# The last row block of a hybrid decoder block: column halves in PSUM tiles of their own, and a planner that takes a PSUM tile as one

## The chip, the cores and the metric

The kernel runs on one core of a Trainium2 chip. Such a core has five engines that run side by side and wait for each other through semaphores: TensorE (PE in the profile, with its weight loads as PEld), VectorE (DVE), ScalarE (ACT), GpSimd (POOL) and SyncE (SP, which here only starts transfers). Matmul results land in PSUM, a small memory of banks; everything else lives in SBUF. The metric is the device time of one execution in microseconds (us). Lower is better.

## The reference

One decoder layer over 1024 positions and 1024 channels, in float32. What matters for the text below is the middle of it:

```python
u = rms_norm(h, mix_pre_g)
z = einsum('bsd,de->bse', u, w_in)            # pooled part, q, k, v, two gates
ya = pool_mixer(p) @ w_branch_a
yb = diff_attention(q, k, v) @ w_branch_b
m = sigmoid(gate_a) * ya + sigmoid(gate_b) * yb
h = h + rms_norm(m @ w_out, mix_post_g)       # "row blocks" below
u = rms_norm(h, ffn_pre_g)
f = silu(u @ w_ffn_gate) * (u @ w_ffn_up)
h = h + rms_norm(f @ w_ffn_down, ffn_post_g)
```

## The kernel before

Every matrix product is made of three matmuls on operands that were split in a high and a low part (`triple`, lines 1056 to 1058: high by high, high by low, low by high), and many are seven-product schemes on 512x512 quarters. In the profile a triple is three rows of PE, one for each of those lines.

The work goes through these stages: the input projection, a part called the mixer (branch A, attention, branch B, the output projection with the residual and the second norm, and the first products of the FFN), the FFN's gate and up products, and the down projection with the last norm.

The mixer is not written in the order in which it runs. `mixer` lists tasks, each with an engine, an estimated duration, the slots it reads (`r=`) and writes (`w=`) and a rank. `Plan.op` makes a graph of them: a task goes behind those that wrote what it reads, and behind those that touched what it writes. A slot may be named with a key, `(o, e)`, and then only tasks with the same key are ordered. For PSUM slots (the pools in `BANKS`: "mm" and "fil" of two tiles of one bank, "pair" of two tiles of two banks) also two readers on different engines are ordered. `Plan.schedule` then gives each engine its order by those estimates, and `Plan.emit` writes the instructions down in the order of the planned starts. The semaphores are not the planner's: the layer below adds them while the instructions are written down, from the tiles that each touches, and it takes a whole tile as one, without the planner's keys. Each engine then works through its list in that order, and an instruction that waits holds all that stand behind it on the same engine.

Two places matter here.

Branch B (`block` and the loop around it, lines 582 to 605). For each of 16 blocks PE makes four triples into a "fil" tile `branch`; DVE multiplies it with a gate (`sgs <- branch, sgs`, after which the bank is free for the block after next) and adds the result to the accumulator `ma`; ahead of that DVE multiplies `ma` with the other gate. For the last four blocks (n of 12 to 15) the gates still need their sigmoid, on ACT, and the first one carries a load of ACT's function table. ACT also splits the branch's weights (`wb_hi`) and DVE makes their low part (`wb_lo`). Then come the weights of the output projection, `wo_raw`, `woh` and `wol`.

The row blocks (`row` for blocks 0 to 6, `last_row` for block 7). PE makes the row block's product `wo` of 128x1024 in a "pair" tile, ACT sums its squares (`sumsq`, into `junk`), DVE multiplies it with the gain (`og`), POOL takes the power for the norm, DVE adds the residual (`xr`), and the same again for the second norm; then PE transposes `og` (`turned`, tile `h_t`), and ACT and DVE make the FFN's operands of it. In blocks 0 to 6 both column halves (e of 0 and 1) are done by one instruction, in block 7 one after the other: eight triples for half 0, then eight for half 1. Between the triples of half 1 PE has the transposes of block 6, and behind them come FFN products (`Y`, `Z`) that need only the first four row blocks, while the norm of block 7 runs on the other engines; then the transposes of block 7.

Of the kernel before, what the change touches and what calls it, by code (L numbers as in the profile page):

```python
# [75 lines left out]
class Plan:  # L76
# [20 lines left out]
    def op(self, engine, cost, fn, r=(), w=(), rank=0.0, size=0.0, claim=(), chain=None, behind=None,  # L97
# [156 lines left out]
def mixer(pl, k):  # L254
# [331 lines left out]
    for n, (d, t) in enumerate(order):  # L586
# [11 lines left out]
        if (1, d) in (k.unfinished if k else [(1, 6), (1, 7)]):  # L598
            pl.op("ACT", act(HALF) + .2, lambda sg=sg: A.activation(sg()[:, 1], sg()[:, 1], AF.Sigmoid),
                  w=[(sg, 1)], rank=r0)  # L600
# [69 lines left out]

    def row_products(o, mh, ml, kb, e, rank):
        hi, lo = wo[kb // 2]

        def fn():
            c = slice(e * HALF, (e + 1) * HALF)
            wh, wl = hi()[:, kb % 2, c], lo()[:, kb % 2, c]
            k.triple(o()[:, e, :], mh()[:, kb, :], ml()[:, kb, :], wh, wl, kb == 0, kb == KD - 1, False)
        return pl.op("PE", TRIPLE, fn, r=[(mh, kb // 2), (ml, kb // 2), (hi, kb % 2), (lo, kb % 2)], w=[(o, e)],
                     rank=rank, chain="fill")

    def turned(tb, og, rank):
        last, h, c = tb == NB - 1, *divmod(tb, 4)
        both = bank("pair", "h_t") if last else None
        for kq in (1, 0) if last else (0, 1):
            pt = both if last else bank("mm", "h_t")
            view = (lambda kq=kq, pt=pt: pt()[:, kq, :]) if last else pt
            key = (pt, kq) if last else (pt, None)

            def fn(kq=kq, view=view):
                for i in range(4):  # L690
                    at = kq * 4 + i
                    nc.tensor.transpose(view()[:, i * P:(i + 1) * P], og()[:, at * P:(at + 1) * P], k.ident)
            done = pl.op("PE", 4 * .109, fn, r=[(og, kq)], w=[key], rank=3000.0)
            v = lambda view=view: view().rearrange("p (k t) -> p k t", k=4)
            src = v, [key], HALF, False
            raw = raws[h][kq]
            if last and kq == 1:
                both_parts(A2, [c], rank - 1, src)
            pl.op("ACT", act(HALF), lambda raw=raw, v=v: A.copy(raw()[:, :, cols(c)], v()), r=[key], w=[(raw, c)],
                  rank=rank)  # L700
# [44 lines left out]
    def last_row():  # L745
        tb, rank = NB - 1, 100.0 + 10 * (NB - 1)
        mh, ml, xr = operands(tb, rank - 18)
        o, og = bank("pair", "wo"), b4([P, D], F32, "og", "row")
        c = [slice(0, HALF), slice(HALF, D)]
        ss, ms, r = small(4, "hss"), small(4, "ms"), small(2, "rstd")  # L750
        for e in range(2):
            for kb in range(KD):
                last7[0] = row_products(o, mh, ml, kb, e, 4000.0 + tb)
            pl.op("ACT", act(HALF) + .23, lambda e=e: k.sumsq(o()[:, e, :], ss()[:, e:e + 1]), r=[(o, e)], w=[(ss, e)],
                  rank=URGENT)
            pl.op("DVE", dve(HALF), lambda e=e: tt(og()[:, c[e]], o()[:, e, :], gpost()[:, c[e]], ALU.mult),
                  r=[(o, e), gpost], w=[(og, e)], rank=URGENT)
        mean(ms, ss, 0, URGENT)
# [959 lines left out]
```

## Time and profile before

| | |
|---|---|
| median of 3 runs | 1254.37 us (1252.97 to 1255.44) |
| the profiled execution | 1254.28 us |
| its span, first to last instruction | 1252.5 us |
| PE busy | 1237.7 us, 99% of the span |
| DVE, ACT, POOL busy | 839.9, 583.9, 142.7 us |
| chain that ended last | PE 95%, DMA 2%, ACT 1%, DVE 1% |

A row of the timeline is: start, duration, engine, source line, instruction, tiles written and read, shapes, count, and in brackets how long the engine had been idle before it and what ended that. Consecutive instructions of one kind are merged to one row. Matmul rows overlap: a row's duration runs to the end of its result, while the next matmul starts earlier. Buffer numbers are left out of the names, so `wo` is the product of any row block and `junk <- wo` any sum of squares over it. `A_lo`, `S_lo`, `A_hi`, `u` around the row blocks are the FFN operands that ACT and DVE make from the transposed rows.

### The profile page before, as it was taken

To read this page: it belongs to the slowest core of one execution; us is meant where nothing else is said; L and a number is where in the kernel's file an instruction comes from. 1 tells how busy PE (TensorE), PEld (TensorE's weight loads), DVE (VectorE), ACT (ScalarE), POOL (GpSimd) and SP (SyncE) were. 2 spreads that over 40 slices of the span, in tenths; PEclk is the share of its full clock that TensorE was granted. 3 is DMA by queue.
4 is the path that set the end of the run, shared out by engine and by line. 5 is a ranking of instruction groups with operands and counts; after the bars stand their busy time and mean duration, and the time that the engine had idled before them with its cause. 6 is when DMAs were issued, how large, how long until landed. Compare 5 with 4: busy or idle time off the path is not lost.

```text
span 1252.5 us, 15725 instructions
## 1 busy us (share of the span) xinstructions
PE 1237.7 (99%) x5900; PEld 1038.0 (83%) x5900; DVE 839.9 (67%) x1314; ACT 583.9 (47%) x1051; POOL 142.7 (11%) x128
## 2 busy tenths in 40 slices
PE   8999999999999999999999999999999999999997
PEld 8888888888899998788788888888888888888886
DVE  5976776445399888885795655655645547955666
ACT  7543344434478773464553333333333333554552
POOL 4100000000201100010002111111111012000222
PEclk9999999999999999999999999999999999999999
DMA  8475336333693027572442332332332368733236
GB/s 253 148 235 192 139 120 221 106 130 118 222 381 136 18 71 266 187 262 89 145 158 87 124 126 85 93 104 98 127 102 98 113 213 278 247 94 107 78 109 210
DMA packets 139548, 190.69 MB, mean 152 GB/s; under 512 B 7632, under 2 KB 90320, under 8 KB 137040
## 3 DMA queue, kind: packets, MB, share of 16 engines
q1 hardware_dynamic: 127904, 159.15, 38.6%
q10 hardware_dynamic: 11568, 30.54, 6.4%
q8 instruction: 46, 0.75, 0.3%
q14 instruction: 30, 0.25, 0.1%
HBM read 128.06 MB, written 61.60 MB: 151 GB/s over the span
## 4 chain that ended last, share of the span: by engine, by line
PE 95%; DMA 2%; ACT 1%; DVE 1%; issue 0%; POOL 0%; SPq 0%; POOLq 0%; DVEq 0%; ACTq 0%
PE Y L1056 10%; PE Y L1058 10%; PE Y L1057 10%; PE X L1056 5%; PE X L1058 5%; PE X L1057 5%; PE Yd L1056 3%; PE Yd L1058 3%; PE Yd L1057 3%; PE Z L1058 3%; PE Z L1056 3%; PE Z L1057 3%; PE s L276 3%; PE o L276 3%; PE wo L1056 2%; PE wo L1058 2%
## 5 line engine op out<-in xcount | busy, mean ns | idle before, releaser
L1007 DVE TENSOR_TENSOR p<-Z,p 128x512 f32<-128x512 f32 x33 | 22.8, 692 | 166.1 <-PE Z L1058 162.5
L1056 PE MATMUL Y<-S_hi,Wh 128*128 128x512 f32 x288 | 112.3, 390 | 0.7 <-ACT p L1092 0.7
L1056 PE MATMUL X<-S_hi,Wh 128*128 128x512 f32 x288 | 112.3, 390 | 0.0
L1058 PE MATMUL Y<-S_hi,Wl 128*128 128x512 f32 x288 | 112.2, 389 | 0.0
L1057 PE MATMUL Y<-S_lo,Wh 128*128 128x512 f32 x288 | 112.1, 389 | 0.0
L1057 PE MATMUL X<-S_lo,Wh 128*128 128x512 f32 x288 | 112.0, 389 | 0.0
L1058 PE MATMUL X<-S_hi,Wl 128*128 128x512 f32 x288 | 112.0, 389 | 0.0
L1056 PE MATMUL Y<-A_hi,Wh 128*128 128x512 f32 x280 | 109.2, 390 | 0.0
L1057 PE MATMUL Y<-A_lo,Wh 128*128 128x512 f32 x280 | 109.1, 390 | 0.0
L1058 PE MATMUL Y<-A_hi,Wl 128*128 128x512 f32 x280 | 108.8, 389 | 0.0
L1025 ACT CAST Wh<-wf_t 128x1024 fp32r<-128x1024 f32 x66 | 68.6, 1053 | 68.1 <-PE Y L1057 32.8
L963 DVE TENSOR_TENSOR Wl<-wf_t,Wh 128x1024 fp32r<-128x1024 f32 x72 | 87.7, 1225 | 7.6 <-ACT Wh L1025 6.3
L963 DVE TENSOR_TENSOR w_op<-wd,w_op 128x512 fp32r<-128x512 f32 x77 | 56.7, 736 | 50.7 <-ACT w_op L1011 50.7
L1025 ACT CAST Wh<-w_raw 128x1024 fp32r<-128x1024 f32 x66 | 55.4, 839 | 67.9 <-PE Z L1057 38.0
L1011 ACT CAST w_op<-wd 128x512 fp32r<-128x512 f32 x77 | 48.0, 623 | 76.4 <-PE Yd L1058 35.1
L963 DVE TENSOR_TENSOR Wl<-w_raw,Wh 128x1024 fp32r<-128x1024 f32 x72 | 68.7, 954 | 16.3 <-ACT Wh L1025 14.7
L1056 PE MATMUL Yd<-w_op,s_op 128*128 128x512 f32 x176 | 68.6, 390 | 0.0
L1057 PE MATMUL Yd<-w_op,s_op 128*128 128x512 f32 x176 | 68.5, 389 | 0.0
L1058 PE MATMUL Yd<-w_op,s_op 128*128 128x512 f32 x176 | 68.3, 389 | 0.0
L1056 PEld LDWEIGHTS Y<-S_hi,Wh 128*128 128x128 f32 x288 | 54.1, 188 | 12.7 <-ACT p L1092 1.1
L1058 PEld LDWEIGHTS X<-S_hi,Wl 128*128 128x128 f32 x288 | 54.1, 188 | 11.2
L1058 PEld LDWEIGHTS Y<-S_hi,Wl 128*128 128x128 f32 x288 | 54.1, 188 | 11.2
(274 smaller groups left out, 3082.0 us busy)
## 6 DMA issues: line engine op xcount, KB each, us to landing
s_raw<-fsd SPq DMA_DIRECT2D x35, 512.0 KB, 3.6
w_raw<-in_w_in_dram SPq DMA_DIRECT2D x32, 512.0 KB, 4.2
w_raw<-in_w_ffn_gate_dram SPq DMA_DIRECT2D x22, 512.0 KB, 3.9
w_raw<-in_w_ffn_up_dram SPq DMA_DIRECT2D x22, 512.0 KB, 3.9
fsd<-fss SPq DMA_DIRECT2D x11, 1024.0 KB, 3.9
wd<-in_w_ffn_down_dram SPq DMA_DIRECT2D x44, 256.0 KB, 5.5
fsd<-F SPq DMA_DIRECT2D x33, 256.0 KB, 2.4
qd<-qk_st ACTq DMA_DIRECT2D x16, 512.0 KB, 4.0
```

Of the source, the lines that this page charges most:

```text
L276: nc.tensor.matmul(o, l, r, start=start, stop=stop, skip_group_check=skip)
L963: nc.vector.tensor_tensor(out=o, in0=a, in1=f32(hi), op=ALU.subtract)
L1007: nc.vector.tensor_tensor(out=o, in0=a, in1=b, op=op)
L1011: nc.scalar.copy(hi, a)
L1025: nc.scalar.copy(hi, a)
L1056: nc.tensor.matmul(o, ah, bh, start=start, stop=False, skip_group_check=goes_on)
L1057: nc.tensor.matmul(o, ah, bl, start=False, stop=False, skip_group_check=goes_on)
L1058: nc.tensor.matmul(o, al, bh, start=False, stop=stop, skip_group_check=goes_on)
```

## The change

Four edits, all in the mixer:

- `Plan.op` drops the key of a slot that lies in PSUM: two tasks on different halves of one PSUM tile are ordered now, as the layer below orders them anyway.
- `last_row` takes two "fil" tiles of one bank each for its two halves, in place of one "pair" tile.
- `turned`, for the last row block, takes a "pair" tile for each of its two groups of four transposes, in place of the two halves of one, and lists both groups ahead of their readers.
- The planned duration of the first sigmoid (n of 12) gets 1.3 us for the table load; the 0.2 us that all four had go.

```diff
         for writes, keys in ((False, r), (True, w)):
             for k in keys:
                 s, key = k if isinstance(k, tuple) else (k, None)
+                key = None if s.pool in BANKS else key
...
-            pl.op("ACT", act(HALF) + .2, lambda sg=sg: A.activation(sg()[:, 1], sg()[:, 1], AF.Sigmoid),
+            pl.op("ACT", act(HALF) + (1.3 if n == 12 else 0), lambda sg=sg: A.activation(sg()[:, 1], sg()[:, 1], AF.Sigmoid),
...
-    def row_products(o, mh, ml, kb, e, rank):
+    def row_products(o, mh, ml, kb, e, rank, both=True):
...
-            k.triple(o()[:, e, :], mh()[:, kb, :], ml()[:, kb, :], wh, wl, kb == 0, kb == KD - 1, False)
+            k.triple(o()[:, e, :] if both else o(), mh()[:, kb, :], ml()[:, kb, :], wh, wl, kb == 0, kb == KD - 1, False)
...
-        both = bank("pair", "h_t") if last else None
-        for kq in (1, 0) if last else (0, 1):
-            pt = both if last else bank("mm", "h_t")
-            view = (lambda kq=kq, pt=pt: pt()[:, kq, :]) if last else pt
-            key = (pt, kq) if last else (pt, None)
-
-            def fn(kq=kq, view=view):
+        order = (1, 0) if last else (0, 1)
+        views = {}
+
+        def turn(kq):
+            pt = bank("pair" if last else "mm", "h_t")
+            view = (lambda: pt()[:, 0, :]) if last else pt
+            views[kq] = pt, lambda: view().rearrange("p (k t) -> p k t", k=4)
+
+            def fn():
...
+        if last:
+            done = [turn(kq) for kq in order][-1]
+        for kq in order:
+            if not last:
+                done = turn(kq)
...
-        o, og = bank("pair", "wo"), b4([P, D], F32, "og", "row")
+        os, og = [bank("fil", "wo") for _ in range(2)], b4([P, D], F32, "og", "row")
...
-                last7[0] = row_products(o, mh, ml, kb, e, 4000.0 + tb)
-            pl.op("ACT", act(HALF) + .23, lambda e=e: k.sumsq(o()[:, e, :], ss()[:, e:e + 1]), r=[(o, e)], w=[(ss, e)],
+                last7[0] = row_products(os[e], mh, ml, kb, e, 4000.0 + tb, False)
+            pl.op("ACT", act(HALF) + .23, lambda e=e: k.sumsq(os[e](), ss()[:, e:e + 1]), r=[os[e]], w=[(ss, e)],
...
-            pl.op("DVE", dve(HALF), lambda e=e: tt(og()[:, c[e]], o()[:, e, :], gpost()[:, c[e]], ALU.mult),
-                  r=[(o, e), gpost], w=[(og, e)], rank=URGENT)
+            pl.op("DVE", dve(HALF), lambda e=e: tt(og()[:, c[e]], os[e](), gpost()[:, c[e]], ALU.mult),
+                  r=[os[e], gpost], w=[(og, e)], rank=URGENT)
```

The order of instructions on ACT, POOL and SP stays as it was, and so does PE's but for the tiles it writes. What changes is the following. In the rows below the last number of a name is the buffer, and the brackets name the engine whose semaphore an instruction waits for.

On PE, at the seam of the two halves of row block 7: the last matmul of half 0, the first triple of half 1 and the beginning of the next ones. Before, all write `wo_5666`:

```order
L1058 MATMUL wo_5666<-woh_5004,ml_5580 128x512
L1056 MATMUL wo_5666<-woh_4850,mh_5574 128x512
L1057 MATMUL wo_5666<-wol_4861,mh_5574 128x512
L1058 MATMUL wo_5666<-woh_4850,ml_5580 128x512
L1056 MATMUL wo_5666<-woh_4850,mh_5574 128x512 [waits Activation_49]
L1057 MATMUL wo_5666<-wol_4861,mh_5574 128x512
L1058 MATMUL wo_5666<-woh_4850,ml_5580 128x512
L1056 MATMUL wo_5666<-woh_4900,mh_5574 128x512 [waits DVE_49]
```

The same place now, where half 1 writes `wo_5705`:

```order
L1067 MATMUL wo_5666<-woh_5010,ml_5580 128x512
L1065 MATMUL wo_5705<-woh_4848,mh_5574 128x512
L1066 MATMUL wo_5705<-wol_4856,mh_5574 128x512
L1067 MATMUL wo_5705<-woh_4848,ml_5580 128x512
L1065 MATMUL wo_5705<-woh_4848,mh_5574 128x512
L1066 MATMUL wo_5705<-wol_4856,mh_5574 128x512
L1067 MATMUL wo_5705<-woh_4848,ml_5580 128x512
L1065 MATMUL wo_5705<-woh_4895,mh_5574 128x512
```

The waits for ACT and for DVE in the second and third triple of half 1 are gone, and no other wait stands in these rows.

On DVE, in branch B around the first of the four sigmoids, before (`branch_4818` and `branch_4840`, now `branch_4841`, are the blocks of n of 8 and 9, `sgs_4754` and `sgs_4773` the gates of n of 13 and 14):

```order
L279 TENSOR_TENSOR sgs_4675<-branch_4795,sgs_4675 128x512
L279 TENSOR_TENSOR ma_4070<-ma_4070,sgs_4754 128x512
L963 TENSOR_TENSOR wb_lo_4833<-wb_raw_4643,wb_hi_4822 128x1024
L279 TENSOR_TENSOR ma_3094<-ma_3094,sgs_4675 128x512
L279 TENSOR_TENSOR sgs_4678<-branch_4818,sgs_4678 128x512
L279 TENSOR_TENSOR ma_4023<-ma_4023,sgs_4773 128x512
L279 TENSOR_TENSOR ma_4023<-ma_4023,sgs_4678 128x512
L963 TENSOR_TENSOR wol_4861<-wo_raw_4799,woh_4850 128x1024
L279 TENSOR_TENSOR sgs_4686<-branch_4840,sgs_4686 128x512
```

And now:

```order
L280 TENSOR_TENSOR sgs_4675<-branch_4795,sgs_4675 128x512
L280 TENSOR_TENSOR ma_4070<-ma_4070,sgs_4754 128x512
L280 TENSOR_TENSOR ma_3094<-ma_3094,sgs_4675 128x512
L280 TENSOR_TENSOR ma_4023<-ma_4023,sgs_4773 128x512
L972 TENSOR_TENSOR wb_lo_4839<-wb_raw_4643,wb_hi_4827 128x1024
L280 TENSOR_TENSOR sgs_4678<-branch_4818,sgs_4678 128x512
L972 TENSOR_TENSOR wol_4856<-wo_raw_4799,woh_4848 128x1024
L280 TENSOR_TENSOR sgs_4686<-branch_4841,sgs_4686 128x512
L280 TENSOR_TENSOR ma_4023<-ma_4023,sgs_4678 128x512
```

`wb_lo` goes behind two updates of `ma`, one of which reads the transferred gate `sgs_4773`, and the multiplication of `branch_4841` ahead of one of them. Some rows further on two more updates of `ma` change places.

On PE, the transposes of row block 7, before:

```order
L1058 MATMUL Y_5808<-A_hi_5180,Wl_5757 128x512
L692 MATMUL h_t_5837<-ident,og_5715 128x128 [waits DVE_49]
L692 MATMUL h_t_5837<-ident,og_5715 128x128 x3
L692 MATMUL h_t_5837<-ident,og_5715 128x128 [waits DVE_49]
L692 MATMUL h_t_5837<-ident,og_5715 128x128 x3
L1056 MATMUL Z_5848<-A_hi_5251,Wh_5752 128x512
```

And now:

```order
L1067 MATMUL Y_5809<-A_hi_5180,Wl_5758 128x512
L695 MATMUL h_t_5838<-ident,og_5716 128x128 [waits DVE_49]
L695 MATMUL h_t_5838<-ident,og_5716 128x128 x3
L695 MATMUL h_t_5845<-ident,og_5716 128x128 [waits DVE_49]
L695 MATMUL h_t_5845<-ident,og_5716 128x128 x3
L1065 MATMUL Z_5850<-A_hi_5251,Wh_5753 128x512
```

The eight transposes stand where they stood, four of them in a second tile.

More of the change, by code (lines that the diff above doesn't have):

```diff
@@ L692, in fn @@
                     nc.tensor.transpose(view()[:, i * P:(i + 1) * P], og()[:, at * P:(at + 1) * P], k.ident)
[L693 to L695 removed]
+            return pl.op("PE", 4 * .109, fn, r=[(og, kq)], w=[pt], rank=3000.0)
+        if last:
[3 more added lines that the diff above has]
+                done = turn(kq)
+            pt, v = views[kq]
+            src = v, [pt], HALF, False
             raw = raws[h][kq]
@@ L698, in turned @@
                 both_parts(A2, [c], rank - 1, src)
-            pl.op("ACT", act(HALF), lambda raw=raw, v=v: A.copy(raw()[:, :, cols(c)], v()), r=[key], w=[(raw, c)],
+            pl.op("ACT", act(HALF), lambda raw=raw, v=v: A.copy(raw()[:, :, cols(c)], v()), r=[pt], w=[(raw, c)],
                   rank=rank)
```

## The prediction

> **What bounds the kernel now.** I read the page's first part, then the list of who waited for whom on PE, then the timeline around each of the places that this list gives. The page says that PE is the bound:
>
> ```profile
> span 1252.5 us, 15725 instructions
> PE 1237.7 (99%) x5900; PEld 1038.0 (83%) x5900; DVE 839.9 (67%) x1314; ACT 583.9 (47%) x1051; POOL 142.7 (11%) x128
> ```
>
> PE idles for 14.8 us in all, and a change that removes no matmul can only gain there. The list of PE's waits names few places; these three lie in the mixer, the others in the head of the program, which the change does not touch:
>
> ```profile
> PE wo L1056 <- ACT junk L1004: 0.9, 1, 0.9
> PE wo L1056 <- DVE ms L640: 0.9, 1, 0.9
> PE branch L1056 <- DVE sgs L279: 0.4, 1, 0.4
> ```
>
> The first two are the seam of the halves in row block 7. Its timeline (PE's weight loads and most matmuls left out):
>
> ```profile
> 607.79 0.39 PE L1058 MATMUL wo<-woh,ml 128*128 128x512 f32 x1
> ...
> 608.19 0.55 POOL L636 TENSOR_TENSOR rstd<-ms,mhalf 128x1 f32<-128x1 f32 x1 [3.41 <-DVE ms L640]
> ...
> 608.47 0.39 PE L1058 MATMUL wo<-woh,ml 128*128 128x512 f32 x1
> 608.97 0.60 ACT L1004 ACTIVATE junk<-wo 128x512 bf16<-128x512 f32 x1 [1.05 <-PE wo L1058]
> 609.47 0.20 ACT L1004 ACTIVATION_READ_ACCUMULATOR junk<-wo 128x1 f32 x1
> ...
> 609.72 0.50 PE L1056 MATMUL wo<-woh,mh 128*128 128x512 f32 x1 [0.86 <-ACT junk L1004]
> ...
> 610.29 0.39 PE L1058 MATMUL wo<-woh,ml 128*128 128x512 f32 x1
> 610.49 1.05 ACT L650 CAST A_hi<-u 128x1024 fp32r<-128x1024 f32 x1 [0.82 <-PE wo L1057]
> 610.78 0.69 DVE L279 TENSOR_TENSOR og<-wo,gpost 128x512 f32<-128x512 f32 x1 [2.68 <-PE wo L1058]
> ...
> 611.45 1.28 DVE L727 SCALAR_TENSOR_TENSOR og<-xr,rstd,gpre 128x1024 f32<-128x1024 f32 x1
> ...
> 611.53 0.50 PE L1056 MATMUL wo<-woh,mh 128*128 128x512 f32 x1 [0.85 <-DVE ms L640]
> ...
> 613.07 1.23 DVE L963 TENSOR_TENSOR A_lo<-u,A_hi 128x1024 fp32r<-128x1024 f32 x1 [0.34 <-PE wo L1057]
> ...
> 613.71 1.03 PE L692 MATMUL h_t<-ident,og 128*128 128x128 f32 x8
> 614.21 1.22 DVE L963 TENSOR_TENSOR S_lo<-u,S_hi 128x1024 fp32r<-128x1024 f32 x1
> 614.35 1.08 ACT L699 COPY u<-h_t 128x512 f32<-128x512 f32 x2 [1.86 <-PE h_t L692]
> ...
> 615.46 0.69 DVE L279 TENSOR_TENSOR u<-u,u 128x512 f32<-128x512 f32 x1
> ```
>
> Half 0 ends with the matmul of 607.79, at 608.18; that of 608.47 ends half 1's first triple. ACT could sum half 0 at 608.18 and begins at 608.97, when the triple of the other half has ended at 608.86. PE's next triple then waits until ACT has read, DVE's `og` of half 0 waits for that triple's end (610.68), and the triple after it waits for `og`. Two halves that share no number hand each other the turn, and the wait is by tile.
>
> **The change, part by part.** *Halves in tiles of their own.* No instruction is added or removed. PE's triples stand 0.68 apart (607.79 to 608.47). Five triples of half 1 stand ahead of the transposes of block 6 in PE's order. With the first ending its issue at 608.47, the second would start at 608.70 and the transposes, four triples later, at 611.42; they started at 613.71. That is 2.29 us, more than the 1.71 of the two waits, because the matmuls after a wait follow more slowly (the two rows of 0.50).
>
> Then something else could be late: the transposes need block 6's `og`. In the new order ACT sums half 0 from 608.29 (0.11 behind the end, as now) to 608.99, since its two rows take 0.70; `og` of half 0, which still waits for ACT because both read one bank, runs from 609.04; the next DVE row of length, that of 611.45, follows 0.67 behind and ends at 610.99. POOL's factor for it is there at 608.74. PE comes at 611.42, so it does not wait, by 0.4 us. ACT's `A_hi` waits for PE's second triple and moves up with it.
>
> Behind this, DVE and ACT must follow by as much as PE, or PE waits later. `A_lo` loses its own wait of 0.34 and starts near 610.95, `S_lo` 1.14 later at 612.09, `u <- u,u` 1.25 later at 613.34 (its copies on ACT end at 611.42 + 0.64 + 1.08 = 613.14). It started at 615.46, so DVE moves up by 2.12, PE by 2.29. The place where the difference counts is the transposes of block 7:
>
> ```profile
> 617.93 0.68 DVE L279 TENSOR_TENSOR og<-wo,gpost 128x512 f32<-128x512 f32 x1
> ...
> 623.49 1.41 DVE L773 SCALAR_TENSOR_TENSOR og<-xr,rstd,gpre 128x512 f32<-128x512 f32 x2
> ...
> 624.81 1.04 PE L692 MATMUL h_t<-ident,og 128*128 128x128 f32 x8
> ...
> 625.88 0.59 ACT L650 CAST A_hi<-h_t 128x512 fp32r<-128x512 f32 x1
> ...
> 627.27 1.08 ACT L699 COPY u<-h_t 128x512 f32<-128x512 f32 x2 [0.32 <-DVE A_lo L963]
> ...
> 631.17 0.39 PE L1056 MATMUL X<-S_hi,Wh 128*128 128x512 f32 x1
> ```
>
> PE's second four start some 0.44 into the row of 624.81, at 625.25, and need DVE's end at 624.90: 0.35 to spare, of which 0.17 goes. No wait, but close. The bounds of this part: the full 2.29 if the norm of block 7 moves up with PE, and 0.35 if it kept its times and PE stood at the transposes instead. I take 2.29, since each link of that chain begins with a wait for PE.
>
> *A tile for each group of transposes.* PE's eight transposes stay together; ACT's and DVE's readers may begin after four. ACT's first reader starts at 625.88, a microsecond behind the first transpose, and was not waiting for them (its row has no bracket), so this gives nothing. It takes both "pair" tiles, one of which `X` needs next: ACT has emptied them at 628.35 (627.27 + 1.08) and `X` starts at 631.17. That covers 2.8 us, and if only PE moved up, 0.5 would be left. The "fil" tiles of the halves are needed next by `Z`: `og` frees the last at 618.61, the `Z` that follows the transposes of 624.81 comes more than 6 us later. Both cost nothing under that cover.
>
> *The planner's key* adds no semaphore; it only makes the plan agree with the tile waits, so its cost is the order that comes out, which is the same on PE, ACT, POOL and SP. In each engine's queue of the row blocks nothing stands behind a new wait.
>
> *The table load counted.* This moves DVE's order in branch B. The rows there:
>
> ```profile
> 490.92 0.52 SPq L363 DMA_DIRECT2D sgs<-sgd  x1
> ...
> 498.90 1.28 ACT L599 ACT_TABLE_LOAD   x1 [5.09 <-DMA sgs<-sgd]
> ...
> 500.21 0.69 DVE L279 TENSOR_TENSOR ma<-ma,sgs 128x512 f32<-128x512 f32 x1
> ...
> 500.73 1.04 ACT L398 CAST wb_hi<-wb_raw 128x1024 fp32r<-128x1024 f32 x1
> ...
> 501.80 1.23 DVE L963 TENSOR_TENSOR wb_lo<-wb_raw,wb_hi 128x1024 fp32r<-128x1024 f32 x1 [0.89 <-ACT wb_hi L398]
> ...
> 503.45 0.39 PE L1058 MATMUL branch<-OTh,wb_lo 128*128 128x512 f32 x1
> 503.55 0.68 DVE L279 TENSOR_TENSOR sgs<-branch,sgs 128x512 f32<-128x512 f32 x1
> ...
> 504.28 0.50 PE L1056 MATMUL branch<-OTh,wb_hi 128*128 128x512 f32 x1 [0.45 <-DVE sgs L279]
> ...
> 507.22 0.50 PE L1056 MATMUL branch<-OTh,wb_hi 128*128 128x512 f32 x1
> ...
> 512.79 0.39 PE L1056 MATMUL branch<-OTh,wb_hi 128*128 128x512 f32 x1
> ```
>
> DVE stands 0.89 idle before `wb_lo`, because ACT is late by the table load, and the multiplication that frees PE's bank (503.55) comes late for it. From 503.45 to 512.79 PE issues 37 matmuls in 9.34 us; at a third of 0.68 each that would be 8.39, so the place costs 0.95, with the slow matmuls at 504.28 and 507.22 in it.
>
> In the new order DVE fills the hole. The addition into `ma` runs at about 500.8, then the multiplication with the third gate, which must have landed:
>
> ```profile
> sgs<-sgd SPq DMA_DIRECT2D x1, 512.0 KB, 10.6
> ```
>
> That is the issue of 490.92 (last column: us to landing), so 501.52. `wb_lo` follows 0.62 later at 502.14 (`wb_hi` ends at 501.77), the multiplication for PE's bank 1.14 behind it at 503.28 in place of 503.55. PE would go on 0.73 later, as now, at 504.01 in place of 504.28; it comes there at 503.68. The stall shrinks by 0.27. The next multiplication now stands behind one `wol` only and not behind two updates, so it is done before 506, while PE comes at 506.9; that saves what 507.22 cost, about 0.2. So 0.47 is gained. Bounds: 0.95 if nothing of the stall is left; a loss of 0.13 or so if the gate lands 0.6 later, since DVE's chain now hangs on that landing.
>
> *The sum.* 2.29 + 0.47 = 2.76 off 1252.5, so a span of 1249.7. The profiled execution took 1254.28, 1.78 more than its span, so 1251.5; the median of the runs shown, 1254.37, is 0.09 above that execution, so 1251.6. By the bounds the gain lies between 0.2 (0.35 - 0.13) and 3.24, 1254.2 to 1251.1.
>
> **The rivals.** *The norm of block 7 does not follow.* PE comes early to block 7's transposes and stands there until DVE's two rows have ended. Against it: the links wait for PE. For it: the slack left is under 0.2, and DVE's rows from 613.07 to 615.46 follow each other without a gap in which a delay could be made up. If the chain moves up half as far, PE waits about 0.8: 1252.4; if not at all, 1253.5. Chance 0.16.
>
> *The branch part gives nothing,* or the gate lands late: 1254.37 - 2.29, 1252.1. Chance 0.15.
>
> *The halves were free of each other all along.* Each half is 128x512 in float32, and if what PE waited for were not the shared tile, splitting it would change nothing: about 1253.9 with the branch part. The Trainium skill, "Perfetto Trace Analysis", section "Matmuls", has independent groups rotate through different banks so that the evacuation of one overlaps the matmuls of the next; by "PSUM — Partial Sum Buffer", section "Specifications (TRN2)", a bank is 512 float32 values, so the halves lay in two banks before and by that rule overlapped already, with nothing to gain. The trace disagrees: PE stood idle 0.86 and 0.85 with the other half being read. Chance 0.03.
>
> *Slower.* The one mechanism I see is the landing of the third gate, with the DMA queue full there. PE's bank now waits for DVE, DVE for `wb_lo`, that for the update, that for the landing. Past 501.5 each microsecond of delay is one of PE's; at 504.3, 13.4 us after the issue, all that both parts gain is eaten, and at 507 the kernel takes 1257. The landing took 10.6 in this execution. Chance 0.03.
>
> **How the numbers follow.** What this kernel's measurement can tell from no change is about 0.2%, 2.5 us, so "faster" begins at 1251.86, just above my time. The forecast has 0.63. Its own range is 1250.9 to 1252.2 and some four fifths of it lie below that bound, 0.50; the branch rival adds a third of its 0.15, the first rival little: faster 0.56. Slower 0.03, and the rest, 0.41, is within 0.2%. The single runs of before spread by 1.2 to either side; with that, and out to the first rival's far end, the range is 1250.2 to 1253.7.
>
> **What the profile of the changed kernel would show.** PE's list of waits has no `wo` row; the DVE row of `og` for half 0 starts under 1 us behind half 0's last matmul; the transposes of block 6 come 3.0 us after half 1's first triple has been issued, and those of block 7 show no wait. DVE has no 0.89 before `wb_lo`, and PE's stall in `branch` is some 0.2. I am wrong if `h_t` stands in PE's list, if `X` or `Z` waits for ACT or DVE, or if the stall in `branch` grows.

## The result, and the profile after

| | before | after |
|---|---|---|
| median, 9 executions each | 1254.05 us (1252.97 to 1255.44) | 1250.68 us (1250.44 to 1251.09) |
| ratio | | 0.9972, 95% interval 0.9962 to 0.9983 |
| the profiled execution, its span | 1254.28, 1252.5 us | 1250.68, 1248.9 us |
| the same kernel again, beside other runs | 1253.45 to 1253.74 (four groups, 102 executions) | 1250.87, ratio 0.9978 (0.9968 to 0.9987) |

The kernel is faster by 0.2 to 0.3%, as forecast, and lower than the 1251.6 that was predicted. To read the medians of before one must know that in 23 of its 102 executions beside the experiments PE's mean granted clock (the share of its full clock that it was allowed) was 0.997 and the time 1254.4 to 1255.9, while the other 79 had 0.998 or more and a mean of 1253.49; that lifts its median by 0.1 to 0.35 and makes most of its spread.

The page's first lines after. PE's idle time, the span less its busy time, falls from 14.8 to 12.9 us:

```profile
span 1248.9 us, 15724 instructions
PE 1236.0 (99%) x5900; PEld 1037.7 (83%) x5900; DVE 839.2 (67%) x1314; ACT 583.5 (47%) x1051; POOL 142.5 (11%) x128
```

Who waited for whom on PE, after. No row of `wo` and none of `branch` is left; what remains lies in the head of the program and in the input projection:

```profile
PE x_t L1217 <- DVE xt L1189: 2.9, 2, 1.6
PE k L1207 <- POOL ident masks.py:199: 1.4, 1, 1.4
PE q L992 <- DVE A_lo L972: 1.3, 2, 0.8
PE Y L1065 <- ACT p L1101: 0.7, 1, 0.7
PE x_t L1217 <- ACT A_raw L1233: 0.3, 1, 0.3
```

The timeline at the seam of the two halves, after. Lines of the changed file lie one to nine further down than before (L1065 to L1067 is the triple, L280 DVE's products and sums, L695 the transposes, L972 the low parts):

```profile
606.47 0.39 PE L1067 MATMUL wo<-woh,ml 128*128 128x512 f32 x1
...
606.98 0.60 ACT L1013 ACTIVATE junk<-wo 128x512 bf16<-128x512 f32 x1 [0.37 <-PE wo L1067]
...
607.15 0.39 PE L1067 MATMUL wo<-woh,ml 128*128 128x512 f32 x1
...
607.70 0.69 DVE L280 TENSOR_TENSOR og<-wo,gpost 128x512 f32<-128x512 f32 x1 [0.91 <-ACT junk L1013]
...
608.37 1.28 DVE L736 SCALAR_TENSOR_TENSOR og<-xr,rstd,gpre 128x1024 f32<-128x1024 f32 x1
...
609.56 1.22 DVE L972 TENSOR_TENSOR A_lo<-u,A_hi 128x1024 fp32r<-128x1024 f32 x1
...
610.11 1.03 PE L695 MATMUL h_t<-ident,og 128*128 128x128 f32 x8
...
611.85 0.69 DVE L280 TENSOR_TENSOR u<-u,u 128x512 f32<-128x512 f32 x1
```

Half 0 ends at 606.86, ACT's sum starts 0.12 later and `og` 0.84 later, where it took 2.60 before. Half 1's first triple has its last matmul at 607.15 and the transposes of block 6 come at 610.11, 2.96 behind it; before it was 5.24 (608.47 to 613.71). So the seam gives 2.28 us.

The end of block 7 in the same timeline:

```profile
619.88 1.41 DVE L782 SCALAR_TENSOR_TENSOR og<-xr,rstd,gpre 128x512 f32<-128x512 f32 x2
...
621.20 1.04 PE L695 MATMUL h_t<-ident,og 128*128 128x128 f32 x8
...
623.21 1.09 ACT L708 COPY u<-h_t 128x512 f32<-128x512 f32 x2
...
627.56 0.39 PE L1065 MATMUL X<-S_hi,Wh 128*128 128x512 f32 x1
```

These transposes come 11.09 behind block 6's, 11.10 before: nothing was given back. DVE's `og` ends at 621.29, the second four need it at 621.64.

Branch B, after:

```profile
497.88 1.28 ACT L600 ACT_TABLE_LOAD   x1 [4.41 <-DMA sgs<-sgd]
...
499.20 2.04 DVE L280 TENSOR_TENSOR ma<-ma,sgs 128x512 f32<-128x512 f32 x3
...
501.16 1.22 DVE L972 TENSOR_TENSOR wb_lo<-wb_raw,wb_hi 128x1024 fp32r<-128x1024 f32 x1
...
502.29 0.69 DVE L280 TENSOR_TENSOR sgs<-branch,sgs 128x512 f32<-128x512 f32 x1
...
503.32 0.39 PE L1065 MATMUL branch<-OTh,wb_hi 128*128 128x512 f32 x1
```

The multiplication that frees PE's bank ends at 502.98, PE takes the bank at 503.32 without a wait, and all of the 0.95 that this place cost in the profiled execution before is gone. But another thing differs too: the first gate landed at 497.88, 5.44 ahead of PE's coming, where it had been 498.90, 4.78 ahead of PE's 503.68. Between the two profiles the span shrank by 3.6: 2.28 at the seam, 0.96 here, and 0.35 in the first 40 us, which the change does not touch. Whether the 0.96 belongs to the change is the question of the first experiments.

### The profile page after: what moved, and what is told of

Read it like the earlier page. It is cut to its first block, busy times and chain, and to the rows that moved or that the text cites. A ratio compares the mean times of both kernels' runs of the same rounds, so it can differ in the third digit from the quotient of the medians.

```text
span 1248.9 us, 15724 instructions
## 1 busy us (share of the span) xinstructions
PE 1236.0 (99%) x5900; PEld 1037.7 (83%) x5900; DVE 839.2 (67%) x1314; ACT 583.5 (47%) x1051; POOL 142.5 (11%) x128
## 4 chain that ended last, share of the span: by engine, by line
PE 96%; ACT 1%; DVE 1%; DMA 0%; issue 0%; POOL 0%; SPq 0%; POOLq 0%; DVEq 0%; ACTq 0%
PE Y L1065 10%; PE Y L1066 10%; PE Y L1067 10%; PE X L1065 5%; PE X L1066 5%; PE X L1067 5%; PE Yd L1065 3%; PE Yd L1066 3%; PE Yd L1067 3%; PE Z L1066 3%; PE Z L1065 3%; PE Z L1067 3%; PE s L277 3%; PE o L277 3%; PE branch L1065 2%; PE branch L1067 2%
## 5 line engine op out<-in xcount | busy, mean ns | idle before, releaser
L1065 PE MATMUL Y<-S_hi,Wh 128*128 128x512 f32 x288 | 112.3, 390 | 0.7 <-ACT p L1101 0.7
L1065 PE MATMUL X<-S_hi,Wh 128*128 128x512 f32 x288 | 112.3, 390 | 0.0
L1067 PE MATMUL Y<-S_hi,Wl 128*128 128x512 f32 x288 | 112.2, 389 | 0.0
L1067 PE MATMUL X<-S_hi,Wl 128*128 128x512 f32 x288 | 112.0, 389 | 0.0
L1065 PE MATMUL Y<-A_hi,Wh 128*128 128x512 f32 x280 | 109.2, 390 | 0.0
L1067 PE MATMUL Y<-A_hi,Wl 128*128 128x512 f32 x280 | 108.8, 389 | 0.0
L972 DVE TENSOR_TENSOR Wl<-wf_t,Wh 128x1024 fp32r<-128x1024 f32 x72 | 87.7, 1225 | 7.8 <-ACT Wh L1034 6.3
L972 DVE TENSOR_TENSOR w_op<-wd,w_op 128x512 fp32r<-128x512 f32 x77 | 56.7, 737 | 50.6 <-ACT w_op L1020 50.6
L972 DVE TENSOR_TENSOR Wl<-w_raw,Wh 128x1024 fp32r<-128x1024 f32 x72 | 68.7, 954 | 16.4 <-ACT Wh L1034 14.6
L1065 PE MATMUL Yd<-w_op,s_op 128*128 128x512 f32 x176 | 68.6, 390 | 0.0
L1067 PE MATMUL Yd<-w_op,s_op 128*128 128x512 f32 x176 | 68.3, 389 | 0.0
L1065 PEld LDWEIGHTS Y<-S_hi,Wh 128*128 128x128 f32 x288 | 54.1, 188 | 12.7 <-ACT p L1101 1.1
L1067 PEld LDWEIGHTS X<-S_hi,Wl 128*128 128x128 f32 x288 | 54.1, 188 | 11.2
L1067 PEld LDWEIGHTS Y<-S_hi,Wl 128*128 128x128 f32 x288 | 54.1, 188 | 11.2
```

What stands on the lines that cost most here:

```text
L972: nc.vector.tensor_tensor(out=o, in0=a, in1=f32(hi), op=ALU.subtract)
L1065: nc.tensor.matmul(o, ah, bh, start=start, stop=False, skip_group_check=goes_on)
L1067: nc.tensor.matmul(o, al, bh, start=False, stop=stop, skip_group_check=goes_on)
```

## Experiments

Times of before stand beside those of the same chip. "Lowest" is the lowest of 10 or 11 executions, and of 15 to 32 for the kernel before. Intervals are of 95%.

**The tiles alone.** The changed kernel with the old cost of the sigmoids:

```diff
-            pl.op("ACT", act(HALF) + (1.3 if n == 12 else 0), lambda sg=sg: A.activation(sg()[:, 1], sg()[:, 1], AF.Sigmoid),
+            pl.op("ACT", act(HALF) + .2, lambda sg=sg: A.activation(sg()[:, 1], sg()[:, 1], AF.Sigmoid),
```

> The changed kernel with the planned cost of the sigmoids put back to 0.2 us each, so that DVE works in branch B in its old order; the PSUM tiles stay as changed. My theory: the tiles are worth 2.3 us by themselves, so 1251.7 beside a kernel before of 1254.0, the waits of `wo` for ACT and DVE are gone, and the stall in `branch` is there as before (0.4 us of wait behind `wb_lo`). Rival 1, the branch's gain in the changed kernel was only luck of the landing and the tiles explain more: 1250.9. Rival 2, without the new order in branch B the later norms come late: 1252.5 to 1253.

Measured: 1251.02 (1250.55 to 1251.53) beside 1253.74, ratio 0.9975 (0.9966 to 0.9984); lowest to lowest, 1252.87 to 1250.55, it is 2.32. The order of instructions on PE, DVE, ACT and POOL is that of the kernel before, so the tiles by themselves do nearly all of it. But no stall was in `branch`, against my expectation, though DVE worked in its old order; the time lies nearer to the first rival's 1250.9 than to my 1251.7:

```profile
497.32 1.28 ACT L600 ACT_TABLE_LOAD   x1 [3.98 <-DMA sgs<-sgd]
...
500.22 1.23 DVE L972 TENSOR_TENSOR wb_lo<-wb_raw,wb_hi 128x1024 fp32r<-128x1024 f32 x1 [0.88 <-ACT wb_hi L399]
...
501.96 0.69 DVE L280 TENSOR_TENSOR sgs<-branch,sgs 128x512 f32<-128x512 f32 x1
...
503.19 0.39 PE L1065 MATMUL branch<-OTh,wb_hi 128*128 128x512 f32 x1
```

The hole of 0.88 is there, and costs PE nothing: the multiplication ends at 502.65 and PE came at 503.19.

**The new order alone.** The kernel before with the new cost of the sigmoids (the diff above the other way round).

> The kernel before with nothing changed but the planned cost of the sigmoids, so that only DVE's order in branch B differs. My theory: the place lost 0.95 us and the new order takes back all or nearly all of it, 0.7 to 0.95 off the kernel before (1253.1 to 1253.3 beside 1254.0), with no wait of `branch` for DVE and the two waits of `wo` unchanged at 0.9 each. Rival, the gain was half of it as predicted, 0.47, and the rest of what the profile showed came from gates that landed early in that one execution: 1253.5, with a stall of some 0.2 left.

Measured: 1253.33 (1252.87 to 1255.04) beside 1253.74, ratio 0.9998 (0.9989 to 1.0007), with both waits of `wo` at 0.86 and 0.85 and no row of `branch`. Neither the 0.7 to 0.95 of my theory nor, by this ratio, anything at all. Of the executions with a granted clock of 0.998 or more, the 8 of this kernel are 0.28 below the 79 of before on the mean (0.07 to 0.50), and 0.26 below the 22 of the same chip (0.02 to 0.50). That is a choice of executions made afterwards, so it is weak evidence.

**The table load taken out of the way.** The kernel before, with a sigmoid of one column behind the last `OTh`, where ACT then stands idle for 7.28:

```diff
+        def head_on():
+            A.mul(dh()[:, h % 2, half(t)], pt()[:, 0, :], k.sgc)
+            if h == NH - 1 and t == 0:
+                A.activation(k.junk[:, :1], k.junk[:, :1], AF.Sigmoid)
...
-        pl.op("ACT", .69, lambda: A.mul(dh()[:, h % 2, half(t)], pt()[:, 0, :], k.sgc), r=[pt], w=[(dh, key)],
+        pl.op("ACT", .69, head_on, r=[pt], w=[(dh, key)],
```

> The kernel before with one more instruction: a sigmoid of one column of the scratch tile `junk`, on ACT directly behind its last `OTh`, so that the function table is loaded while ACT has some 7 us of nothing to do. DVE's order stays the old one. My theory is that the table load between the gate's landing and `wb_hi` is what makes DVE late for PE: without it `wb_hi` ends 1.28 earlier, the hole of 0.89 before `wb_lo` closes and PE's stall with it, so 0.7 to 0.95 off the kernel before, as much as the new order gives. Rival, DVE's old order is late for PE by itself (two updates of `ma` stand ahead of the multiplication) or the gate's landing decides: under 0.3 off.

Measured: 1253.46 (1252.83 to 1254.94) beside 1253.74, ratio 0.9999 (0.9991 to 1.0008). The load did move, and the hole closed:

```profile
484.99 1.28 ACT L559 ACT_TABLE_LOAD   x1
...
498.35 0.63 ACT L604 ACTIVATE sgs<-sgs 128x512 f32<-128x512 f32 x1 [5.05 <-DMA sgs<-sgd]
...
500.27 1.22 DVE L968 TENSOR_TENSOR wb_lo<-wb_raw,wb_hi 128x1024 fp32r<-128x1024 f32 x1
```

`wb_lo` starts 1.92 behind the landing and without a wait, where it took 2.90. It still gives no time that can be told, which is the rival's side (under 0.3): what it removes is not what PE usually waits for.

**The kernel before once more.** No edit.

> The kernel before unchanged, as a measure of what this comparison can tell and of how much one profiled execution differs from another: a ratio of 1.000 with an interval of about 0.001 to either side. In the profile the two waits of `wo` should be 0.9 each again, since they hang on nothing outside; the stall in `branch` should be there with a different size (0.2 to 1 us), if it hangs on when the gates land, and the first 40 us may differ by some tenths.

Measured: 1253.52 (1252.91 to 1254.93), ratio 1.000 (0.9991 to 1.0009). The two waits of `wo` are 0.86 and 0.85 again. `branch` has no row in PE's list:

```profile
497.56 1.28 ACT L599 ACT_TABLE_LOAD   x1 [4.27 <-DMA sgs<-sgd]
...
500.45 1.22 DVE L963 TENSOR_TENSOR wb_lo<-wb_raw,wb_hi 128x1024 fp32r<-128x1024 f32 x1 [0.88 <-ACT wb_hi L398]
...
502.20 0.68 DVE L279 TENSOR_TENSOR sgs<-branch,sgs 128x512 f32<-128x512 f32 x1
...
503.14 0.40 PE L1056 MATMUL branch<-OTh,wb_hi 128*128 128x512 f32 x1
```

So the stall that the prediction was worked out from is not in every execution of the kernel before: of its two profiles one has it, the one in which the gates landed late. How many executions have it, the times do not tell. From the gate's landing to the end of the multiplication the old order takes 5.33 there (498.90 to 504.23), 5.32 here and 5.33 with the tiles alone; what varies is when the gate lands. It landed late because it was issued late. SP issues eight other gates and two gains ahead of it; from the first of these to this gate's issue it took 9.93 there (478.32 to 488.25), 9.12 here (477.80 to 486.92) and 8.78 with the tiles alone (477.86 to 486.64). What slows SP's issues in one execution and not in another, the runs do not show.

**The changed kernel once more.** No edit.

> The changed kernel unchanged, on the same chip as the two others of this call: 1250.7, no wait of `wo` or `branch` in PE's list. The run with the tiles alone took 1251.02 (1250.55 to 1251.53) and its profile shows no stall in `branch`, with DVE's hole of 0.88 before `wb_lo` still there. My theory, corrected by that: in most executions the old order's hole lies within PE's slack and the new order gives 0 to 0.3. Then this kernel's median lies 0 to 0.3 below that of the tiles alone, and its lowest execution at the same 1250.5. Rival: the new order is worth 0.5 or more in every execution, and its lowest execution lies at 1250.0 or below.

Measured: 1250.87 (1250.63 to 1251.47), ratio 0.9978 (0.9968 to 0.9987), and no wait of `wo` or `branch`. Together with the first nine executions the changed kernel has a mean of 1250.85, 0.20 below that of the tiles alone (-0.06 to 0.47, and partly on other chips), and about the same lowest execution (1250.44 and 1250.63, against 1250.55). The rival, half a microsecond in each execution, falls.

**The transposes' tiles undone.** The changed kernel with the old `turned` and without the planner's line:

```diff
-                key = None if s.pool in BANKS else key
...
+        both = bank("pair", "h_t") if last else None
+        for kq in (1, 0) if last else (0, 1):
+            pt = both if last else bank("mm", "h_t")
```

> The changed kernel with the old `turned` (both groups of transposes of block 7 in the two halves of one tile) and without the line in `Op` that drops the key; the halves of block 7 keep their own tiles and the sigmoid its new cost. PE's, DVE's and POOL's order is that of the changed kernel, ACT copies two `h_t` in the other order. My theory: the transposes' tiles and the key are worth nothing by themselves, so this takes what the changed kernel takes, within 0.2 us, and `X` and `Z` wait for nobody. Rival: readers of the first four transposes now wait for the second four, ACT's chain behind them is 0.5 us later, and something of it reaches PE: 0.3 to 1 us slower than the changed kernel with a wait of `X` for ACT.

Measured: 1250.87 (1250.63 to 1251.34), ratio 0.9977 (0.9967 to 0.9986), the same as the changed kernel, with no new wait in PE's list. These two parts are worth nothing beside the other two. The planner's line by itself changes no instruction of the changed kernel; its order without that line is the same on every engine.

**The planner's line alone.** The kernel before, its shared tiles, and the line that drops the key.

> The kernel before with the one line that drops the key of PSUM slots: the tiles stay shared, but the planner knows that the halves order each other. It then puts the `og` of half 0 ahead of half 1's first triple, which waits for DVE, and the transposes of block 6 behind half 1's third triple; the second four transposes of block 7 go four triples later. My theory is that the shared tile costs PE one wait in place of two: half 0 ends, ACT's sum takes 0.80 from there and `og` 0.75 more, so a wait of some 1.6, with one refill of 0.14 where there were two. So 0.3 to 0.6 off the kernel before, 1253.2 to 1253.5 beside 1253.7, and far from the changed kernel: knowing the wait helps little, removing it does. Rival 1: the planner's better order hides the wait behind other work and gives 1.5 us or more. Rival 2: the longer single wait makes the norm of block 7 late, PE waits at its transposes, and it is slower than before by 0.3 or more.

Measured: 1254.63 (1254.00 to 1255.39) beside 1253.61, ratio 1.0006 (0.9997 to 1.0015); lowest to lowest it is 1.16 slower, and on the mean of the executions with a clock of 0.998 or more 1.28 (0.98 to 1.58). Neither my 0.3 to 0.6 nor the first rival; the number is the second rival's, slower by 0.3 or more. Its PE rows in the row blocks with a wait, from the timeline:

```profile
608.80 0.50 PE L1057 MATMUL wo<-woh,mh 128*128 128x512 f32 x1 [1.58 <-DVE ms L641]
...
630.22 0.50 PE L1057 MATMUL X<-S_hi,Wh 128*128 128x512 f32 x1 [0.18 <-ACT S_hi L651]
...
631.37 0.50 PE L1058 MATMUL X<-S_lo,Wh 128*128 128x512 f32 x1 [0.65 <-DVE S_lo L964]
```

The one wait of 1.6 is as expected. But the rest of the loss does not come from PE waiting at the transposes, as that rival had it: the planner moved the second four transposes of block 7 behind five `Z` triples, the operands made from them are late for `X`, and PE waits 0.83 there. From half 0's last matmul to the first `Y` behind `X` it takes 27.17 (606.83 to 634.00), before 26.10 (607.79 to 633.89): 1.07 more. A plan that knows of a wait can still pay for it.

**Late gates, in both orders.** One more transfer on SP, 512 KB inside the device's memory, ahead of the gate of n of 12 (or of 14, with that number in the edit), in the kernel with the tiles alone and in the changed one. The order of all other instructions stays:

```diff
+        def fetch(d=d, t=t, sg=sg, n=n):
+            if n == 12:
+                nc.sync.dma_start(k.spare[:], k.sgd[0][:, :, half(0)])
+            nc.sync.dma_start(sg(), k.sgd[d][:, :, half(t)])
```

> The kernel with the tiles alone (DVE's old order in branch B) and one transfer more: 512 KB from one place of the device's memory to another, issued by SP ahead of the gate of n of 12, so that the gates of n of 12, 13 and 14 land later by some D, which I estimate at 1.5 to 3 us from the 10.6 us that a gate takes there. My theory: in the old order the multiplication that frees PE's bank ends 5.35 us behind the landing of the first of these gates (table load, sigmoid, `wb_hi`, `wb_lo`, an update, the multiplication) and PE came 5.9 behind it in the run without the delay, so PE stalls in `branch` by D - 0.5, 1 to 2.5 us: 1252.0 to 1253.5. Rival: the stall of the kernel before had nothing to do with the landing, PE waits 0.2 or less and the time stays at 1251.0.

Measured: 1252.08 (1251.80 to 1253.02). The profiled execution, at 1253.02 the slowest of the ten, has two stalls. One of 0.21 is a bank earlier (501.14), because DVE itself stands 1.36 for the late gate; the other is the one of the kernel before:

```profile
499.83 1.28 ACT L603 ACT_TABLE_LOAD   x1 [6.19 <-DMA sgs<-sgd]
...
504.47 0.68 DVE L280 TENSOR_TENSOR sgs<-branch,sgs 128x512 f32<-128x512 f32 x1
...
505.20 0.50 PE L1068 MATMUL branch<-OTh,wb_hi 128*128 128x512 f32 x1 [1.05 <-DVE sgs L280]
```

The multiplication ends 5.32 behind the landing, as always in the old order, and PE stalls by what it is ahead of that: my theory, at the low end of its range.

> The same extra transfer at the same place in the changed kernel. My theory: the new order hangs on the third of these gates, which lands some 2.6 behind the first; the multiplication ends 0.65 + 1.14 + 0.69 behind it, 5.1 behind the first, so it stalls D - 0.75 and gains only 0.25 on the old order at the same delay, 0.5 with the second multiplication, as the prediction had it. Rival: the new order fills all of the hole of 0.88 and stalls 0.9 less or more.

Measured: 1251.92 (1251.27 to 1252.94).

```profile
498.74 1.28 ACT L603 ACT_TABLE_LOAD   x1 [5.27 <-DMA sgs<-sgd]
...
501.73 0.69 DVE L280 TENSOR_TENSOR ma<-ma,sgs 128x512 f32<-128x512 f32 x1 [0.39 <-DMA sgs<-sgd]
...
503.48 0.69 DVE L280 TENSOR_TENSOR sgs<-branch,sgs 128x512 f32<-128x512 f32 x1
...
504.22 0.50 PE L1068 MATMUL branch<-OTh,wb_hi 128*128 128x512 f32 x1 [0.73 <-DVE sgs L280]
```

Here DVE waits 0.39 for the third gate, and the multiplication ends 2.44 behind it; that is 5.43 behind the first, no earlier than in the old order. With all gates late the two orders take about the same, 1252.08 and 1251.92. Their means lie 0.19 apart (-0.26 to 0.65), which leaves room for the 0.25 to 0.5 of my theory and none for the 0.9 of the rival.

> The kernel with the tiles alone and the extra transfer ahead of the gate of n of 14 only. My theory: the old order needs this gate only behind the multiplication of the bank that PE takes next, so it stalls little, under 0.7: 1251.0 to 1251.7. Rival: as much as with all three late.

Measured: 1251.20 (1250.72 to 1252.15), 0.2 above the run without the transfer, as expected of the old order.

```profile
498.79 1.28 ACT L603 ACT_TABLE_LOAD   x1 [4.91 <-DMA sgs<-sgd]
...
503.43 0.69 DVE L280 TENSOR_TENSOR sgs<-branch,sgs 128x512 f32<-128x512 f32 x1
...
504.17 0.50 PE L1068 MATMUL branch<-OTh,wb_hi 128*128 128x512 f32 x1 [0.28 <-DVE sgs L280]
```

Even this stall comes from the first gate, which is 5.33 ahead of the multiplication's end and landed late by itself in that execution: it was issued at 488.20, ahead of the added transfer (490.85).

> The changed kernel with the extra transfer ahead of the gate of n of 14 only. My theory, the slower rival of the prediction: the multiplication that frees PE's bank now stands behind `wb_lo`, and that behind the update that reads this gate, so PE stalls by D less a slack of 0.3 to 0.8, 0.7 to 2.5 us, more than the old order with the same transfer: 1251.5 to 1253.3. Rival: DVE has the slack and the time stays at 1250.8.

Measured: 1252.18 (1251.41 to 1252.90), 1.3 above the changed kernel and 1.0 above the old order with the same transfer; by the means it is 1.2 and 0.7 (0.27 to 1.21). Its profiled execution, 1251.43, is nearly the fastest of the ten:

```profile
497.64 1.28 ACT L603 ACT_TABLE_LOAD   x1 [4.05 <-DMA sgs<-sgd]
...
501.48 0.69 DVE L280 TENSOR_TENSOR ma<-ma,sgs 128x512 f32<-128x512 f32 x1 [1.30 <-DMA sgs<-sgd]
...
503.23 0.68 DVE L280 TENSOR_TENSOR sgs<-branch,sgs 128x512 f32<-128x512 f32 x1
...
503.96 0.50 PE L1068 MATMUL branch<-OTh,wb_hi 128*128 128x512 f32 x1 [0.36 <-DVE sgs L280]
```

DVE stands 1.30 for the third gate and PE waits 0.36 for DVE. So the new order exchanges one dependence for another: the first gate's landing plus 5.33 for the third gate's plus 2.43. In the changed kernel's own profile the third row of the three updates at 499.20 starts at 500.55 (499.20 + 2.04 - 0.69) and the multiplication ends 2.43 behind that, which makes 5.10 from the first gate: 0.23 better than the old order. That third gate was issued at 489.92 and takes 10.6, so the row starts as the gate lands: even without a delay the new order hangs on it, and its 0.23 holds only while the third gate lands 2.67 or less behind the first.

**The two waits put back, without a shared tile.** In the changed kernel half 1 lies in a two-bank tile of its own, and ACT and DVE each write one column into its second bank, which no matmul uses:

```diff
+        seven = bank("pair", "wo")
+        os, og = [bank("fil", "wo"), seven], b4([P, D], F32, "og", "row")
...
+            def total(e=e):
+                if e == 0:
+                    A.copy(seven()[:, 1, :1], k.seen[0])
+                k.sumsq(half_of(os[e], e), ss()[:, e:e + 1])
...
+            def gain(e=e):
+                if e == 0:
+                    V.tensor_copy(seven()[:, 1, 1:2], k.seen[1])
+                tt(og()[:, c[e]], half_of(os[e], e), gpost()[:, c[e]], ALU.mult)
```

> The changed kernel with the two waits put back and nothing shared: half 1 of block 7 lies in the first half of a two-bank tile of its own, and into the unused second half ACT writes one column ahead of its sum over half 0, DVE one column ahead of its multiplication of half 0. The order on every engine is that of the changed kernel but for these two small copies (about 0.2 us each), and PE's second and third triple of half 1 wait for ACT and DVE as in the kernel before. My theory: the two waits alone make what the tiles gave, 2.29 plus 0.2 to 0.4 for the copies, so the lowest execution at 1252.9 to 1253.3 beside 1250.6 of the changed kernel, and waits of `wo` of 0.9 to 1.1 each. Of the executions so far, about one in four of the kernels with these two waits had a granted clock of 0.997 and a time above 1254.2, and none of those without; if that belongs to the waits, two to four of some eleven executions lie 1.2 to 2 above the lowest here too. Rival: what the tiles gave came from the order around them or from the pools, and the waits are hidden elsewhere: under 1252.0.

Measured: 1252.13 (1251.48 to 1252.47), 1.3 above the changed kernel, half of what I expected; the lowest execution even lies where the rival had it, under 1252.0. The rows say why:

```profile
607.08 0.39 PE L1078 MATMUL wo<-woh,ml 128*128 128x512 f32 x1
...
607.50 0.16 ACT L769 COPY wo<-seen 128x1 f32<-128x1 f32 x1 [0.97 <-PE wo L1078]
...
607.72 0.50 PE L1076 MATMUL wo<-woh,mh 128*128 128x512 f32 x1 [0.25 <-ACT wo L769]
...
608.78 0.16 DVE L774 COPY wo<-seen 128x1 f32<-128x1 f32 x1 [2.07 <-PE wo L1078]
...
609.00 0.50 PE L1076 MATMUL wo<-woh,mh 128*128 128x512 f32 x1 [0.32 <-DVE wo L774]
...
611.21 1.03 PE L698 MATMUL h_t<-ident,og 128*128 128x128 f32 x8
```

The edit missed its aim: the small copies stand ahead of the sum and the multiplication, and PE goes on as soon as a copy of 0.16 is done, not after 0.6 to 0.7. So the waits are not hidden elsewhere, as the rival has it, but short. And the run gives a second point for the price. From the last matmul of half 1's first triple (607.08) to the transposes of block 6 it takes 4.13, which is 1.17 more than the 2.96 of the changed kernel, with 0.57 of waits; before it was 2.28 more with 1.71. Both times two waits cost 0.57 to 0.60 beyond their brackets, 0.29 to 0.30 each. The halves shared no number, no bank and no tile here, and but for the copies the order was the same: the waits alone make the cost. They also show that the semaphores go by the tile, since PE waited for copies into a bank that it does not write. The granted clock of 0.997, which I had thought possible, came in none of the 11 executions; with waits this short that does not say whether long ones bring it.

## Why the prediction was right, and where a size was off

*Halves in tiles of their own: right, in mechanism and size.* Predicted were 2.29 us and transposes 3.0 behind the first triple; measured 2.28 and 2.96 in the profile, 2.32 between the lowest executions, and 2.44 between the means (1253.49 to 1251.05). `og` of half 0 came 0.84 behind the matmul, under the 1 us named. The run with the waits put back gives nearly the same behind each wait, 0.30 for 0.29, so the step's remark that the loss exceeds the two brackets holds with a number. It nearly holds elsewhere: with the planner's line alone, three waits of 1.58, 0.18 and 0.65 with 0.29 each would make 3.28, 0.99 more than the 2.29 of before; the rows show 1.07 more, so 0.32 each.

*One remark of the prediction does not hold:* that PE idles for 14.8 us and only there something can be gained. Of the 3.6 that the span shrank, 1.7 lies in PE's busy time (1237.7 to 1236.0, with 5900 instructions in both). Of the 2.28 at the seam 0.57, and of the 0.96 in branch B some 0.5, are matmuls that no longer follow a wait more slowly, and such rows count as busy. The sum did not use the remark.

*The first rival, that the norm of block 7 does not follow,* falls: the distance from block 6's transposes to block 7's is 11.09 after 11.10, with 0.35 to spare on DVE. The prediction had DVE follow by 2.12 only and 0.17 of that slack go; `u <- u,u` starts 1.74 behind the transposes of block 6 where it started 1.75 behind, so nothing of it went. The copies left the tiles at 624.30 (623.21 + 1.09) and `X` began at 627.56.

*The rival that the halves were free of each other all along* falls with the first experiment. The Trainium skill, "Perfetto Trace Analysis", section "Matmuls", asks that independent groups rotate through different banks; the halves did so before, in two banks, and PE idled 0.86 and 0.85. The measurement decides: separate banks were not enough, it took separate tiles, because the semaphores are set by the tile, as the run with the waits put back shows.

*A tile for each group of transposes, and the planner's key: right, both nothing.* Of the key the prediction said that its cost is the order that comes out; on the old tiles that order was a loss of 1.0 to 1.3.

*The table load counted: the mechanism was right, the size was taken from an execution that was not typical.* This step gave 0.47, from a stall of 0.95. The stall is that of one profiled execution; in the second profile of the same kernel and in that of the tiles alone the old order stalls nowhere, with the same hole before `wb_lo`. Its own arithmetic stands: the multiplication was to move up by 0.27, and the rows after give 0.23. What the step missed is that in those two profiles PE comes 0.26 and 0.54 after the old order has freed the bank (502.88 to 503.14, 502.65 to 503.19), so that what the order saves is slack there. Measured over executions, the order is worth 0.20 (-0.06 to 0.47) with the new tiles and 0.28 (0.07 to 0.50) with the old ones, so little that it may be nothing. The profile after was to show a stall of some 0.2 and showed none, because its gates landed 0.66 earlier ahead of PE (5.44 against 4.78), not because the order did more. The rival that this part gives nothing was as good a forecast.

*The slower rival,* a late third gate, did not occur, but its mechanism is real: with that gate delayed, the changed kernel loses 1.3 us and the old order 0.2 by the medians.

*The sum.* Predicted 2.76. Over executions with a granted clock of 0.998 or more it is 2.64 (1253.49 to 1250.85, interval 2.47 to 2.80), over all of them 2.99. That 2.64 comes so near to 2.76 is partly luck: the tiles gave 2.44 for 2.29, the order about 0.2 for 0.47, and the two errors offset each other. The medians of 1254.05 and 1250.68 differ by more, 3.37, because of the executions of before at 0.997 and of nine draws. The forecast of the time hangs on the median that it starts from: 1251.6, from a median of 1254.37, came out 0.9 too high, and that median of three lay 0.6 to 0.9 above those of the four larger groups.

## What to carry to other kernels

Look for PE waits between tasks that share no number: a tile framework that orders by the tile makes two column halves in one PSUM tile take turns even in separate banks, and each such wait cost its bracket plus about 0.3 us of slower matmuls behind it here, so the price can be read from the timeline before the edit. Price a stall that hangs on a transfer from several profiled executions, and by the distance from the landing to the freed bank (here 5.33 in five executions of four kernels) against when PE comes, not from the bracket of one. And telling a planner of a wait does not remove it: the same line of the plan lost 1.0 to 1.3 us on the shared tiles and changes nothing on separate ones.

## What the runs showed of the hardware

ACT's table load, which waits for the gate of n of 12, starts 10.64 to 10.68 us behind that gate's issue in four executions (488.25 to 498.90, 487.21 to 497.88, 486.64 to 497.32, 486.92 to 497.56); what moved between executions, by up to 1.6, was the issue. The Trainium skill, "ScalarE: Activation LUTs", section "What ACT_TABLE_LOAD costs", gives 1283 ns for the load and about 1380 ns for a drain. The load's rows of 1.28 agree; a drain is not to be seen here, since the sigmoid starts 1.29 behind the load's start (497.32 to 498.61 in the run with the tiles alone).

A mean granted clock of 0.997 was recorded in 30 of 135 executions of the kernels with both long waits of `wo` (the kernel before, the new order alone, the early table load, the kernel before once more), and in none of 101 of the others (19 of the changed kernel, 10 each of the tiles alone and of the transposes undone, 40 with a late gate, 11 with short waits put back, and 11 of the planner's line, which has one wait of 1.58). The 30 took 1.5 us longer than the 105 on the mean. That they go with the waits is seen; why, no run here shows, since no profiled execution was one of them: in the profiles of the kernel before the granted clock reads 1.00 in every stretch of 20 us up to 1240.
